# A decoder block in float32 pairs: right-hand SBUF pools moved from 96 to 64 bytes past multiples of 128, and the squares of the residual written two tiles back

## The chip, the cores and the metric

The kernel runs on one core of one Trainium2 chip. Its time is device microseconds from start to end of one execution; the number given for a kernel is the median of several executions. Engines are named as in the profile: PE multiplies matrices (PEld loads its stationary operand), DVE and ACT work element by element, POOL and SP mostly issue DMAs here.

## The reference

One layer of a decoder block, 512 tokens by 2048 features, all float32:

```python
h = rms_norm(x, g_mix)
x = x + concat(rms_norm(nsa(h)), gla(h)) @ w_out
x = x + cross_attention(rms_norm(x, g_cross), rms_norm(mem, g_mem)) @ w_co   # 4 heads, 256 memory tokens
hf = rms_norm(x, g_ffn)                                  # this x is "x2" below
gg, uu = split(hf @ w_gu)                                # 2048 -> 2 * 5632
return x + (silu(gg) * uu) @ w_down                      # 5632 -> 2048
```

## The kernel before

Every product that matters is a three-part product: each float32 operand is split into a high part (ACT, `S.copy` to fp32r) and a low part (DVE, source minus high part), in `split` (L186 and L187), and `mm3` issues three matmuls of 128x128 by 512 columns: high stationary with high moving, the same stationary with low moving, low stationary with high moving. This document calls these three a **triple**. All are recorded on L107. In a tile list such as `t<-qh,PB` the first name is the PSUM bank, the second the moving operand, the third the stationary one.

The stages, in order: projections of `mem` and `x` (`natural`, where the weights move and the tiles `X` are stationary; `project`, where the weights `wh`, `wl` are stationary and `X` moves), the attention groups, `w_out`, cross attention, then per 128-feature tile m the `w_co` product (`co_part`, both operands in right-hand pools), then the gate and up product in Strassen form (`phase`, `product`: split weights `qh`, `ql` move and the prepared activations `PA`, `PB` are stationary), and the down product (`down_product`, again `qh`, `ql` moving over `PB`).

SBUF is given out from both ends. Pools opened on the left (`const`, `sbb`, later `PA`, `PB`, `C`) start at multiples of 128 bytes in each partition, and so do nearly all their tiles; `X`, `PA`, `PB`, `C` all do. Pools opened with `side="right"` grow down from the top: first `sba` (`wh`, `wl`, `w`, `KS`, `KV`, `on`, `q1`, `rs`, `M`), later, in its place, the pool of `T2`, `qh`, `raw`, `ql`. By the sizes of the small tiles at the top, these tiles all start 96 bytes past a multiple of 128. So the two operands of a matmul start either 96 bytes (`qh` over `PB`) or 32 bytes (`X` over `wh`) apart, modulo 128, or at the same place (`M` over `wh`, both right; `P` over `Q` in cross attention, both left).

The stage around the second edit is the loop over the 16 tiles m of x2 (L1163 on). Tile m of the residual lies in `xs[m]`; which right-hand buffer that is, `X_AT` says. Per m: `co_part` on PE; DVE adds the residual into `xs[m]` (L1170); ACT's queue issues the store of `xs[m]` to DRAM (L1173); ACT scales it by the gain into half of a `PB` tile (`begin_combos`, L1111). Every second m, DVE and ACT build the sums and splits of that pair (`sums`, L1123 to L1126, then `split`), and PE does `unsummed`, 12 matmuls, for the pair before. `square(m - 2)` (L1157) squares `xs[m-2]` in place on ACT, which must wait until the store has read the tile, and POOL adds the square to one of two DRAM accumulators, `ssd`, by an accumulating DMA (L1159, L1161); each such DMA waits for the one before it on the same accumulator. Squares 14 and 15 come after the loop.

Then `first.close()` gives the right-hand buffers to `raw`, `qh` and `ql`, so that the first loads and splits of the FFN wait for what last used those bytes: the third `raw` tile lies over the buffers of x2's tiles 14 and 15. `phase` begins with a head: the weights of two slices, kp = 0 and 1, are loaded, and their products are written bank set by bank set, for each set first kp = 0 and then kp = 1. Instructions are ordered by a scheduler with priorities, so written order and engine order differ; the rows below are from the engine order.

Of the kernel before, what the change touches and what calls it, by code (L numbers as in the profile page):

```python
# [13 lines left out]
AF = mybir.ActivationFunctionType  # L14
OP = mybir.AluOpType
# [4 lines left out]
KT = D // 128  # L20
# [4 lines left out]
KP = KT // 2  # L25
NB = D_FF // 512
AHEAD = 150
# [16 lines left out]

FIRST_SUM, LAST_SUM = 70, 576

X_AT = ("KV", (3, 14, 12, 7, 13, 15, 2, 1, 0, 8)), ("KS", (11, 4, 5, 6)), ("q1", (9,)), ("on", (10,))
OC = "M", "M", "on", "KV"

SV = {}  # L50
# [10 lines left out]
def hybrid_block(ctx: ExitStack, tc: tile.TileContext, x_t, mem_t, sv, cmat, umask, w_a, w_r67, w_v, w_vg, w_v3,  # L61
                 w_vsw, w_gk2, w_c1, w_c2, w_out, w_cq, w_ck, w_cv, w_co, w_gu, w_down, y_t):
    nc = tc.nc
    V, S, G, PE = nc.vector, nc.scalar, nc.gpsimd, nc.tensor
# [11 lines left out]
    def sb(shape, tag, bufs, dt=F32):  # L76
        return (pool_b if tag in LATE else pool).tile(shape, dt, name=tag, tag=tag, bufs=bufs)
# [18 lines left out]
    def bank(tag):  # L96
        return psp.tile([128, 512], F32, name=tag, tag=tag, bufs={"mm": 3, "s": 2, "t": 2, "o": 1}[tag])
# [3 lines left out]
    def row(tag, dt=F32):  # L101
        return sb([128, 512], tag, BUFS[tag], dt)
# [125 lines left out]
    def mm3(ps, lhs, rhs, start, stop, again=False):  # L228
        mm(ps, lhs[0], rhs[0], start=start, stop=False, skip_group_check=again)
        mm(ps, lhs[0], rhs[1], start=False, stop=False, skip_group_check=again)  # L230
        mm(ps, lhs[1], rhs[0], start=False, stop=stop, skip_group_check=again)
# [255 lines left out]
    rs, rc = norm["row"], norm["col"]  # L487
# [480 lines left out]
    xs = [None] * KT  # L968
    for tag, ms in X_AT:
        for m in ms:  # L970
# [4 lines left out]
    for m in range(KT):  # L975
# [13 lines left out]
        else:  # L989
            sq = row("n")  # L990
# [73 lines left out]
    def co_part(ps, m, hs):  # L1064
        for h in hs:
            mm3(ps, co[m // 2](512 * (m % 2) + 128 * h, 128), oc[h], start=h == 0, stop=h == 3)

    co = [Weights(w_co[c], 1024, ahead=60) for c in range(2)]
    flows.until(lambda: len(oc) >= 3)
    ps4 = [bank(t) for t in ("mm", "mm", "mm", "s")]  # L1070
# [4 lines left out]
    flows.drain()  # L1075
    held.close()

    BUFS2 = {"T2": 8, "raw": 3, "qh": 5, "ql": 4, "PA": 16, "PB": 17, "C": 8}
    COLS2 = {"raw": 2048, "qh": 1024, "ql": 1024, "PB": 1280}
    pools2 = {}  # L1080

    def open_pool(names, **side):
        p = ctx.enter_context(tc.tile_pool(name="s" + names[0], bufs=1, reuse_waits="tile", **side))
        for n in names:
            pools2[n] = p
            sb2(n)

    def sb2(tag, dt=F32):
        return pools2[tag].tile([128, COLS2.get(tag, 512)], dt, name=tag, tag=tag, bufs=BUFS2[tag])

# [11 lines left out]
    ssd = [dram.tile([128, 512], F32, name="ss", tag="ss", bufs=2) for _ in range(2)]  # L1102
# [29 lines left out]
    def factor(kp, a, i):  # L1132

        return part(combos[kp][a > 1], 256 * (0, 1, 3, 4, 0, 1, 2)[a] + 128 * i, 128)

    def product(banks, kp, a, w, start, stop, again):
        for i in range(2):
            mm3(banks[i], factor(kp, a, i), w, start=start, stop=stop, again=again)
# [13 lines left out]
    def unsummed(kp):  # L1152
        for banks, a in ((b1, 0), (bp, 1)):
            product(banks, kp, a, wa[kp][a], kp == 0, kp == KP - 1, False)

    def square(m):
        S.activation(xs[m], xs[m], AF.Square)  # L1157
        if m < 2:
            G.dma_start(ssd[m], xs[m])  # L1159
        else:  # L1160
            G.dma_start(ssd[m % 2], xs[m], accum_op=OP.add)  # L1161

    for m in range(KT):  # L1163
        x = xs[m]
        if m < 4:
            ps = ps4[m]
        else:
            ps = bank("mm")
            co_part(ps, m, range(4))
        V.tensor_add(x, ps, x)  # L1170
        if m % 4 == 0:
            x2d.append(dram.tile([128, 2048], F32, name="x2", tag="x2", bufs=4))
        S.dma_start(x2d[-1][:, 512 * (m % 4):512 * (m % 4) + 512], x)  # L1173
        if m % 2 and m < 13:
            co.append(Weights(w_co[m // 2 + 2], 1024, ahead=60))
        begin_combos(m, x)
        if m % 2:
            wa[m // 2] = weights_a(m // 2)
            if m > 2:
                unsummed(m // 2 - 1)  # L1180
                sums(m // 2 - 1)()
        if m > 1:
            square(m - 2)
    for m in (KT - 2, KT - 1):
        square(m)
    unsummed(KP - 1)
    sums(KP - 1)()

    first.close()
    open_pool(("T2", "qh", "raw", "ql"), side="right")  # L1190
    open_pool(("C",))
    kept = [None] * KP

# [34 lines left out]
    PHASE_1 = (4, 0, 5, 3)  # L1228
    PHASE_2 = (1, 2, 6)

    def phase(load, banks, plan, middle, last, fresh, ahead, extra, fence=()):

        ws = {}

        def weights(kp):
            with tc.high_priority(offset=AHEAD if kp > 1 else ahead), ExitStack() as behind:
                if kp == 2:
                    for i in fence:
                        behind.enter_context(tc.issue_after(i.ins))
                ws[kp] = load(kp)  # L1240

        for kp in range(2):
            weights(kp)
        for p, a in enumerate(plan):
            for kp in range(2):
                product(banks[p], kp, a, ws[kp][p], fresh and kp == 0, False, not fresh)
        for kp in range(2, KP):
            weights(kp)
            for p in last if kp == KP - 1 else middle:
                product(banks[p], kp, plan[p], ws[kp][p], False, kp == KP - 1, not fresh)  # L1250
            for go in extra.get(kp, ()):
                go()
# [43 lines left out]
    fence = ()  # L1296
    for n in range(NB):
        if n == 0:
            u, c11 = [sb2("C") for _ in range(2)], [sb2("C") for _ in range(2)]
            with tc.high_priority(offset=2 * EVICT):  # L1300
                for i in range(2):
                    fa = S.copy(u[i], b1[i])
                for i in range(2):
                    fv = V.tensor_add(c11[i], u[i], bp[i])
            bu, b2, b3 = [bank("mm"), bank("mm")], [bank("mm"), bank("o")], [bank("t"), bank("t")]
            phase(weights_b, (bu, b2, b3), (4, 5, 3), (1, 2, 0), (0, 1, 2), True, AHEAD, {KP - 3: [norm_2]}, (fa, fv))
        else:
            b1 = c11 = [bank("mm"), bank("mm")]
            bu = [bank("s"), bank("s")]
            b2 = [bank("t"), bank("t")]  # L1310
            b3 = [bank("mm"), bank("o")]
            phase(lambda kp: weights_1(n, kp), (bu, b1, b2, b3), PHASE_1, (2, 3, 1, 0), (1, 0, 2, 3), True, AHEAD, {},
                  fence)
            u = [sb2("C") for _ in range(2)]
        c22 = [sb2("C") for _ in range(2)]
        with tc.high_priority(offset=EVICT):
            for i in range(2):
                if n:
                    fa = S.copy(u[i], b1[i])
                V.tensor_sub(u[i], u[i], bu[i])  # L1320
            for i in range(2):
                V.tensor_add(c22[i], u[i], b2[i])
            for i in range(2):
                fv = V.tensor_add(c22[i], c22[i], b3[i])
        extra = {}
        if hs:
            extra = {2: [turn(hs, n - 1, 0)], 4: [turn(hs, n - 1, 1)]}
        if n == 0:
            phase(weights_c, (b2, b3), (2, 6), (0, 1), (0, 1), False, AHEAD, {}, (fv,))
        else:  # L1330
            phase(lambda kp: weights_2(n, kp), (b1, b2, b3), PHASE_2, (1, 0, 2), (0, 1, 2), False, AHEAD, extra,
                  (fa, fv))
        g1, g2 = [sb2("C") for _ in range(2)], [sb2("C") for _ in range(2)]
        with tc.high_priority(offset=EVICT):
            for i in range(2):
                fa = S.activation(g1[i], c11[i], AF.Silu, scale=rc2[0][:, i:i + 1])
            for i in range(2):
                V.tensor_add(g2[i], u[i], b2[i])
            for i in range(2):
                fv = V.tensor_add(u[i], u[i], b3[i])  # L1340
        fence = fa, fv
        for i in range(2):
            S.activation(g2[i], g2[i], AF.Silu, scale=rc2[0][:, 2 + i:3 + i])
        for i in range(2):
            V.scalar_tensor_tensor(g1[i], u[i], rc2[1][:, i:i + 1], g1[i], op0=OP.mult, op1=OP.mult)
        for i in range(2):
            V.scalar_tensor_tensor(g2[i], c22[i], rc2[1][:, 2 + i:3 + i], g2[i], op0=OP.mult, op1=OP.mult)
        hs = g1 + g2
# [87 lines left out]
    banks = [None, [bank(t) for t in SETS[1]]]  # L1436
# [3 lines left out]
    for step, plan in enumerate(STEPS):  # L1440
# [3 lines left out]
        elif step == 1:  # L1444
            banks = [[bank(t) for t in SETS[r]] for r in rs_]
        elif step == 2:
            banks[1] = [bank(t) for t in SETS[1]]
        else:
            banks = [[bank(t) for t in SETS[r]] for r in rs_]
        for kp in range(NK):  # L1450
# [13 lines left out]
            if step == 0 and kp % 2 and 5 <= kp < 21:  # L1464
                for m in (kp - 5, kp - 4):
                    if m % 4 == 0:
                        raw = sb1("raw")
# [139 lines left out]
```

## Time and profile before

| what | us |
|---|---|
| median of 3 executions | 2365.82 (2364.24 to 2371.68) |
| the profiled execution | 2368.13 |
| its span, first to last instruction | 2366.3 |
| PE idle in front of matmuls, longest | 5.49, at 1057.9 |

The page of the profile gives busy time by engine, the chain of waits that ended last, and the costliest groups of instructions. A matmul's record lasts about 0.4 us, but the next one starts before it ends; the distance between the starts of neighbours, called **pitch** here, is what adds up to time. It is read from the timeline, whose first column is the start in us from the start of the span. The timeline merges equal neighbours into one row with a count.

### The profile page before, as it was taken

To read this page: it belongs to the slowest core of one execution; us is meant where nothing else is said; L and a number is where in the kernel's file an instruction comes from. 1 tells how busy PE (TensorE), PEld (TensorE's weight loads), DVE (VectorE), ACT (ScalarE), POOL (GpSimd) and SP (SyncE) were. 2 spreads that over 40 slices of the span, in tenths; PEclk is the share of its full clock that TensorE was granted. 3 is DMA by queue.
4 is the path that set the end of the run, shared out by engine and by line. 5 is a ranking of instruction groups with operands and counts; after the bars stand their busy time and mean duration, and the time that the engine had idled before them with its cause. 6 is when DMAs were issued, how large, how long until landed. Compare 5 with 4: busy or idle time off the path is not lost.

```text
span 2366.3 us, 29749 instructions
## 1 busy us (share of the span) xinstructions
PE 2345.7 (99%) x10962; PEld 1913.9 (81%) x10962; DVE 1663.5 (70%) x2523; ACT 1179.9 (50%) x1793; POOL 149.9 (6%) x200
## 2 busy tenths in 40 slices
PE   8999999999999999989999999999999999999999
PEld 7898887888887888778888888888888888878787
DVE  6637885666778335586788778878877876775685
ACT  6533454556667224474455444544554555444442
POOL 0011111111112110020000000000000000000000
PEclk9999999999999999999999999999999999999999
DMA  7487568865558773296345435544554397776773
GB/s 272 151 209 177 139 160 223 211 171 136 163 143 253 213 180 114 84 228 206 129 159 182 153 122 170 169 148 136 166 168 144 134 317 281 237 236 228 241 248 143
DMA packets 140995, 434.72 MB, mean 184 GB/s; under 512 B 14416, under 2 KB 34896, under 8 KB 137392
## 3 DMA queue, kind: packets, MB, share of 16 engines
q1 hardware_dynamic: 88528, 329.25, 41.9%
q0 software_dynamic: 28896, 79.18, 15.6%
q10 hardware_dynamic: 23424, 24.39, 3.0%
q8 instruction: 86, 1.41, 0.3%
q14 instruction: 61, 0.50, 0.1%
HBM read 394.22 MB, written 101.45 MB: 209 GB/s over the span
## 4 chain that ended last, share of the span: by engine, by line
PE 97%; DVE 1%; DMA 1%; ACT 1%; issue 0%; SPq 0%; DVEq 0%; ACTq 0%
PE mm L107 51%; PE t L107 18%; PE s L107 15%; PE o L107 10%; PE t L894 1%; PE s L1265 1%; DMA PH<-w_ck 0%; PE t L1415 0%; DMA st<-x_t 0%; DVE ql L187 0%; DMA st<-w_gk 0%; DMA ss<-KV 0%; PE t L882 0%; ACT PB L186 0%; DVE ss L467 0%
## 5 line engine op out<-in xcount | busy, mean ns | idle before, releaser
L186 ACT CAST qh<-raw 128x1024 fp32r<-128x1024 f32 x498 | 481.4, 976 | 545.8 <-PE o L107 177.6
L187 DVE TENSOR_TENSOR ql<-raw,qh 128x1024 fp32r<-128x1024 f32 x498 | 558.2, 1127 | 194.5 <-PE mm L107 46.9
L107 PE MATMUL mm<-X,wh 128*128 128x512 f32 x1664 | 533.8, 401 | 0.0
L107 PEld LDWEIGHTS mm<-X,wh 128*128 128x128 f32 x1664 | 305.8, 189 | 66.0 <-issue 1.7
L107 PE MATMUL t<-qh,PB 128*128 128x512 f32 x968 | 339.1, 395 | 0.0
L107 PE MATMUL mm<-X,wl 128*128 128x512 f32 x832 | 330.3, 397 | 0.0
L187 DVE TENSOR_TENSOR wl<-w,wh 128x1024 fp32r<-128x1024 f32 (+2 forms) x172 | 205.9, 1202 | 158.9 <-ACT wh L186 157.0
L107 PE MATMUL mm<-qh,PB 128*128 128x512 f32 x868 | 314.9, 395 | 0.0
L186 ACT CAST wh<-w 128x1024 fp32r<-128x1024 f32 (+2 forms) x172 | 176.3, 1030 | 265.4 <-PE mm L107 170.1
L107 PE MATMUL s<-qh,PB 128*128 128x512 f32 x672 | 235.7, 395 | 0.0
L107 PE MATMUL mm<-qh,PA 128*128 128x512 f32 x640 | 224.3, 394 | 0.0
L107 PEld LDWEIGHTS t<-qh,PB 128*128 128x128 f32 x968 | 181.8, 188 | 44.5
L107 PEld LDWEIGHTS mm<-qh,PB 128*128 128x128 f32 x868 | 163.7, 189 | 40.7 <-ACT qh L186 0.4
L107 PE MATMUL o<-qh,PB 128*128 128x512 f32 x484 | 190.1, 394 | 5.5 <-ACT qh L186 5.5
L107 PE MATMUL t<-ql,PB 128*128 128x512 f32 x484 | 192.8, 398 | 0.0
L107 PEld LDWEIGHTS mm<-X,wl 128*128 128x128 f32 x832 | 156.6, 188 | 37.7 <-DVE wl L187 1.2
L107 PE MATMUL mm<-ql,PB 128*128 128x512 f32 x434 | 173.1, 399 | 1.0 <-DVE ql L187 1.0
L107 PEld LDWEIGHTS s<-qh,PB 128*128 128x128 f32 x672 | 126.2, 188 | 30.7
L107 PEld LDWEIGHTS mm<-qh,PA 128*128 128x128 f32 x640 | 120.2, 188 | 29.9
L107 PE MATMUL s<-ql,PB 128*128 128x512 f32 x336 | 133.9, 398 | 0.2 <-DVE ql L187 0.2
L107 PE MATMUL mm<-ql,PA 128*128 128x512 f32 x320 | 127.5, 399 | 0.0
L107 PEld LDWEIGHTS o<-qh,PB 128*128 128x128 f32 x484 | 91.0, 188 | 28.5 <-ACT qh L186 5.9
(456 smaller groups left out, 3431.6 us busy)
## 6 DMA issues: line engine op xcount, KB each, us to landing
raw<-w_gu SPq DMA_DIRECT2D x80, 768.0 KB, 4.2
raw<-w_down SPq DMA_DIRECT2D x88, 512.0 KB, 4.6
raw<-w_gu SPq DMA_DIRECT2D x80, 512.0 KB, 3.6
td<-w_down POOLq DMA_DIRECT2D x66, 512.0 KB, 7.1
w<-w_a SPq DMA_DIRECT2D x60, 512.0 KB, 5.4
raw<-td SPq DMA_DIRECT2D x22, 1024.0 KB, 4.8
PB<-h SPq DMA_DIRECT2D x35, 512.0 KB, 4.3
h<-T ACTq DMA_DIRECT2D x66, 256.0 KB, 3.6
```

The lines of the kernel that those rows point to most:

```text
L107: last_mm[0] = PE.matmul(*args, **kw)
L186: S.copy(hi, src)
L187: V.tensor_sub(lo, src, hi)
L894: PE.transpose(tp[:, 128 * (i - j):128 * (i - j) + 128], ps_[b][:, POFF[i] + 128 * j:POFF[i] + 128 * j + 128], ident)
L1265: PE.transpose(ps[f][:, 128 * i:128 * i + 128], hs[i][:, c:c + 128], ident)
```

## The change

Four edits. `pad` is a tile of 32 bytes in each of the two right-hand pools; it is never written or read, and lets everything below it start 64 bytes past a multiple of 128 instead of 96. `square(m)` runs in iteration m itself and writes into the buffer of tile m-2 (for m = 0 and 1 into a free row). `X_AT` exchanges the buffers of tiles 12 to 15, so that the third `raw` tile now lies over tiles 12 and 13, into which squares 14 and 15 go. In the first FFN phase alone, the head goes through all three bank sets for kp = 0 and then for kp = 1 (`by_pair`).

```diff
-X_AT = ("KV", (3, 14, 12, 7, 13, 15, 2, 1, 0, 8)), ("KS", (11, 4, 5, 6)), ("q1", (9,)), ("on", (10,))
+X_AT = ("KV", (3, 12, 14, 7, 15, 13, 2, 1, 0, 8)), ("KS", (11, 4, 5, 6)), ("q1", (9,)), ("on", (10,))
...
+    sb([128, 8], "pad", 1)
     co = [Weights(w_co[c], 1024, ahead=60) for c in range(2)]
...
-    BUFS2 = {"T2": 8, "raw": 3, "qh": 5, "ql": 4, "PA": 16, "PB": 17, "C": 8}
-    COLS2 = {"raw": 2048, "qh": 1024, "ql": 1024, "PB": 1280}
+    BUFS2 = {"T2": 8, "raw": 3, "qh": 5, "ql": 4, "PA": 16, "PB": 17, "C": 8, "pad": 1}
+    COLS2 = {"raw": 2048, "qh": 1024, "ql": 1024, "PB": 1280, "pad": 8}
...
     def square(m):
-        S.activation(xs[m], xs[m], AF.Square)
+        sq = xs[m - 2] if m > 1 else row(("rs", "q1")[m])
+        S.activation(sq, xs[m], AF.Square)
         if m < 2:
-            G.dma_start(ssd[m], xs[m])
+            G.dma_start(ssd[m], sq)
         else:
-            G.dma_start(ssd[m % 2], xs[m], accum_op=OP.add)
+            G.dma_start(ssd[m % 2], sq, accum_op=OP.add)
...
-        if m > 1:
-            square(m - 2)
-    for m in (KT - 2, KT - 1):
         square(m)
...
-    open_pool(("T2", "qh", "raw", "ql"), side="right")
+    open_pool(("T2", "qh", "raw", "ql", "pad"), side="right")
...
-        for p, a in enumerate(plan):
-            for kp in range(2):
-                product(banks[p], kp, a, ws[kp][p], fresh and kp == 0, False, not fresh)
+        head = [(p, kp) for p in range(len(plan)) for kp in range(2)]
+        for p, kp in sorted(head, key=lambda h: h[1]) if by_pair else head:
+            product(banks[p], kp, plan[p], ws[kp][p], fresh and kp == 0, False, not fresh)
```

ACT at the end of the loop over m, before; `KV_7114` and `KV_7122` hold tiles 14 and 15, `PB_9303` and `PB_9371` are the last two pairs, `C` the first evictions of the FFN:

```order
L1111 ACTIVATE PB_9371<-KV_7114,vecs_113 128x512
L1157 ACTIVATE KV_7116<-KV_7116 128x512
L1173 DMA x2_9301<-KV_7122 128x512
L1111 ACTIVATE PB_9371<-KV_7122,vecs_113 128x512
L1157 ACTIVATE KV_7120<-KV_7120 128x512
L186 CAST PA_9391<-PB_9371 128x512
L186 CAST PB_9418<-PB_9303 128x1280
L1157 ACTIVATE KV_7114<-KV_7114 128x512
L1157 ACTIVATE KV_7122<-KV_7122 128x512
L186 CAST PB_9444<-PB_9371 128x1280
L1302 COPY C_9466<-t_8912 128x512
L1302 COPY C_9467<-t_8913 128x512
```

The same place now; `KV_7116` and `KV_7120` hold tiles 14 and 15, `PB_9310` and `PB_9378` are the last two pairs:

```order
L1159 ACTIVATE KS_7132<-KV_7122 128x512
L1175 DMA x2_9308<-KV_7116 128x512
L1112 ACTIVATE PB_9378<-KV_7116,vecs_113 128x512
L1159 ACTIVATE KV_7114<-KV_7116 128x512
L1175 DMA x2_9308<-KV_7120 128x512
L1112 ACTIVATE PB_9378<-KV_7120,vecs_113 128x512
L186 CAST PB_9425<-PB_9310 128x1280
L186 CAST PA_9398<-PB_9378 128x512
L1159 ACTIVATE KV_7122<-KV_7120 128x512
L186 CAST PB_9447<-PB_9378 128x1280
L1301 COPY C_9470<-t_8913 128x512
L1301 COPY C_9471<-t_8914 128x512
```

Two squares fewer stand between the last scaled tile and the last cast, the last square no longer overwrites the tile that was just sent to DRAM, and the wide cast of pair 6 now stands ahead of the cast of pair 7.

PE in the head of the first FFN phase, before; `qh_9486`, `ql_9487`, `qh_9482`, `ql_9483` are weights of kp = 0, `qh_9496` and `ql_9497` of kp = 1:

```order
L107 MATMUL mm_9474<-ql_9487,PB_8983 128x512
L107 MATMUL mm_9474<-qh_9486,PB_8984 128x512
L107 MATMUL mm_9475<-ql_9487,PB_8983 128x512
L107 MATMUL mm_9475<-qh_9486,PB_8984 128x512
L107 MATMUL mm_9474<-qh_9496,PB_9058 128x512
L107 MATMUL mm_9475<-qh_9496,PB_9058 128x512
L107 MATMUL mm_9476<-ql_9483,PB_8983 128x512
L107 MATMUL mm_9474<-ql_9497,PB_9058 128x512
```

The same place now; `qh_9490`, `ql_9491`, `qh_9486`, `ql_9487` are weights of kp = 0, `qh_9500` of kp = 1:

```order
L107 MATMUL mm_9480<-qh_9486,PB_8991 128x512
L107 MATMUL o_9481<-ql_9487,PB_8990 128x512
L107 MATMUL o_9481<-qh_9486,PB_8991 128x512
L107 MATMUL t_9482<-qh_9486,PB_8990 128x512
L107 MATMUL t_9482<-ql_9487,PB_8990 128x512
L107 MATMUL t_9482<-qh_9486,PB_8991 128x512
L107 MATMUL t_9483<-qh_9486,PB_8990 128x512
L107 MATMUL t_9483<-ql_9487,PB_8990 128x512
L107 MATMUL t_9483<-qh_9486,PB_8991 128x512
L107 MATMUL mm_9478<-qh_9500,PB_9065 128x512
```

The first matmul that needs kp = 1 has moved from the ninth place of the head to the nineteenth.

More of the change, by code (lines that the diff above doesn't have):

```diff
@@ L1229, in hybrid_block, with phase @@
     PHASE_2 = (1, 2, 6)
-    def phase(load, banks, plan, middle, last, fresh, ahead, extra, fence=()):
+    def phase(load, banks, plan, middle, last, fresh, ahead, extra, fence=(), by_pair=False):
         ws = {}
@@ L1305, in hybrid_block @@
             bu, b2, b3 = [bank("mm"), bank("mm")], [bank("mm"), bank("o")], [bank("t"), bank("t")]
-            phase(weights_b, (bu, b2, b3), (4, 5, 3), (1, 2, 0), (0, 1, 2), True, AHEAD, {KP - 3: [norm_2]}, (fa, fv))
+            phase(weights_b, (bu, b2, b3), (4, 5, 3), (1, 2, 0), (0, 1, 2), True, AHEAD, {KP - 3: [norm_2]}, (fa, fv),
+                  True)
         else:
```

## The prediction

> **What bounds the kernel now.** The page first: the span, the busy time of PE, and the chain that ended last.
>
> ```profile
> span 2366.3 us, 29749 instructions
> PE 2345.7 (99%) x10962; PEld 1913.9 (81%) x10962; DVE 1663.5 (70%) x2523; ACT 1179.9 (50%) x1793; POOL 149.9 (6%) x200
> PE 97%; DVE 1%; DMA 1%; ACT 1%; issue 0%; SPq 0%; DVEq 0%; ACTq 0%
> ```
>
> PE is busy from end to end and carries 97% of the chain, so waits can give back about 20 us at most. More can come only from the pitch of the matmuls. The timeline gives it; in each pair of rows below I count the matmuls from the first start to the second.
>
> ```profile
> 1232.52 0.39 PE L107 MATMUL t<-qh,PB 128*128 128x512 f32 x1
> 1239.52 0.39 PE L107 MATMUL s<-qh,PB 128*128 128x512 f32 x1
> ...
> 849.77 0.63 PE L107 MATMUL mm<-X,wh 128*128 128x512 f32 x2
> 857.51 0.63 PE L107 MATMUL mm<-X,wh 128*128 128x512 f32 x2
> ...
> 1034.53 0.61 PE L107 MATMUL mm<-KV,wh 128*128 128x512 f32 x2
> 1037.25 0.61 PE L107 MATMUL mm<-KV,wh 128*128 128x512 f32 x2
> ```
>
> In the FFN (right-hand moving operand, left-hand stationary one, 96 bytes apart modulo 128), 30 matmuls take 7.00 us: 0.700 us for a triple. In the projections (left moving, right stationary, 32 apart), 33 take 7.74: 0.7036 for a triple. In the `w_co` stage (both right-hand, 0 apart), 12 take 2.72: 0.680 for a triple. All have 512 columns. So where the two operands start at the same place modulo 128, a triple is 20 to 24 ns shorter. Is that something else, such as other engines or DMAs at work beside it? Two stretches of the FFN, by windows (columns: stretch, length, busy time and count of PE, PEld, DVE, ACT, POOL, clock, DMA share, GB/s):
>
> ```profile
> 1225.00:1250.00 25.00, 25.00 (x108) 20.10 (x108) 16.44 (x21) 9.58 (x13) 0.00 (x0) 1.00 0.28 95
> 2050.00:2075.00 25.00, 25.00 (x108) 20.10 (x108) 17.71 (x15) 11.50 (x11) 0.00 (x0) 1.00 0.74 248
> ```
>
> DMA share 0.28 or 0.74, the same 108 matmuls: the pitch does not follow the traffic. It belongs to the operands' placement, and the first edit alters exactly that.
>
> **The pad.** It adds no instruction. Everything right-hand moves from 96 to 64 bytes past a multiple of 128; left-hand tiles stay. Pairs that lay 96 or 32 apart now lie 64 apart; pairs within one side stay 0 apart. How many triples that touches is read from the groups, where a triple has two matmuls with the high moving or stationary part (`qh`, `wh`):
>
> ```profile
> L107 PE MATMUL t<-qh,PB 128*128 128x512 f32 x968 | 339.1, 395 | 0.0
> L107 PE MATMUL mm<-qh,PB 128*128 128x512 f32 x868 | 314.9, 395 | 0.0
> L107 PE MATMUL s<-qh,PB 128*128 128x512 f32 x672 | 235.7, 395 | 0.0
> L107 PE MATMUL mm<-qh,PA 128*128 128x512 f32 x640 | 224.3, 394 | 0.0
> L107 PE MATMUL o<-qh,PB 128*128 128x512 f32 x484 | 190.1, 394 | 5.5 <-ACT qh L186 5.5
> L107 PE MATMUL mm<-X,wh 128*128 128x512 f32 x1664 | 533.8, 401 | 0.0
> L107 PE MATMUL mm<-wh,X 128*128 128x512 f32 x224 | 80.8, 403 | 6.2 <-ACT wh L186 6.0
> L107 PE MATMUL o<-wh,X 128*128 128x512 f32 x96 | 39.1, 407 | 0.0
> ```
>
> FFN and down product: (968 + 868 + 672 + 640 + 484) / 2 = 1816 triples. `X` over `wh`: 832. `wh` over `X`: (224 + 96) / 2 = 160, taken like the FFN.
>
> No row shows two operands 64 apart, so the new pitch has to be bounded. The nearest rows are 0 apart (0.680) and 32 or 96 apart (0.700, 0.7036). Downwards, a triple could come to 0.680: 1976 x 0.020 + 832 x 0.0236 = 39.5 + 19.6 = **59 us** gained. In the middle, 64 apart could cost what 32 and 96 cost: nothing gained. Upwards, the cost could grow with the distance, 64 being as far as two places modulo 128 can be: twice the excess, 59 us lost. I take the lower bound, 59 us gained. The reason is what the excess does at 0, 32 and 96: none, 24 ns and 20 ns. If operands are read in pieces of 64 bytes, both neighbours of 0 are half a piece out of step, and 64 is in step again, like 0. The size fits: 20 ns a triple is 6.7 ns a matmul, and from the next rows 256 more columns take 226.7 - 118.3 = 108.4 ns, so that 16 columns, which are 64 bytes, take 6.8. Against it stand the same rows, with 256 columns, where placement hardly matters:
>
> ```profile
> 983.64 1.59 PE L107 MATMUL s<-P,Q 128*128 128x256 f32 x12
> 985.06 0.40 PE L107 MATMUL mm<-M,wh 128*128 128x512 f32 x1
> ...
> 112.11 0.40 PE L107 MATMUL t<-wh,X 128*128 128x256 f32 x2
> 113.91 0.28 PE L107 MATMUL t<-wh,X 128*128 128x256 f32 x1
> ```
>
> Both left-hand: 12 in 1.42 us, 118 ns each; 96 apart: 15 in 1.80, 120 ns each. So I count nothing for narrower matmuls, and the middle bound keeps a real chance.
>
> DVE and ACT have 30% and 50% of the span free; a PE that is 2.5% faster raises DVE from 70% to 72%. In the FFN window above DVE has 16.44 of 25 us, so the splits keep ahead. I count no new waits.
>
> The Trainium skill's page "SBUF — State Buffer", section "Who interferes with whom", gives PE two independent read ports, one for the moving operand and one for the weights, and says that PE never waits on anyone. By that, placement could not matter and this edit would give nothing, which is the first rival below. The rows of this trace, 0.680 beside 0.700 for equal shapes, speak against it.
>
> **The squares, `X_AT` and the head.** They act at one place, the handover to the FFN, where PE has its longest idle time. The timeline there:
>
> ```profile
> 1047.54 0.72 ACT L1111 ACTIVATE PB<-KV,vecs 128x512 f32<-128x512 f32 x1 [1.48 <-DVE PB L1123]
> 1048.69 0.60 ACT L186 CAST PA<-PB 128x512 fp32r<-128x512 f32 x1
> 1049.19 1.26 ACT L186 CAST PB<-PB 128x1280 fp32r<-128x1280 f32 x1
> 1052.04 0.40 PE L107 MATMUL s<-wh,PA 128*128 128x512 f32 x1
> 1050.73 0.42 DVE L1126 TENSOR_TENSOR PB<-PB 128x256 f32<-128x256 f32 x1
> 1054.17 0.63 ACT L1157 ACTIVATE KV<-KV 128x512 f32<-128x512 f32 x1 [3.19 <-DMA x<-KV]
> 1054.71 1.24 ACT L186 CAST PB<-PB 128x1280 fp32r<-128x1280 f32 x1
> 1055.86 1.06 ACT L1302 COPY C<-t 128x512 f32<-128x512 f32 x2
> 1055.98 1.49 DVE L187 TENSOR_TENSOR PB<-PB 128x1280 fp32r<-128x1280 f32 x1 [3.42 <-ACT PB L186]
> 1056.81 3.04 ACT L186 CAST qh<-raw 128x1024 fp32r<-128x1024 f32 x4
> 1057.39 1.28 DVE L1304 TENSOR_TENSOR C<-C,s 128x512 f32<-128x512 f32 x2
> 1057.92 0.80 PE L107 MATMUL o<-qh,PB 128*128 128x512 f32 x1 [5.49 <-ACT qh L186]
> 1058.59 3.56 DVE L187 TENSOR_TENSOR ql<-raw,qh 128x1024 fp32r<-128x1024 f32 x4
> 1060.46 0.79 PE L107 MATMUL mm<-ql,PB 128*128 128x512 f32 x1 [0.38 <-DVE ql L187]
> 1061.29 7.78 SPq L1216 DMA_DIRECT2D raw<-gu  x4
> ```
>
> ACT stands 3.19 us before square 15, which may not overwrite tile 15 until its store has read it. Behind it in ACT's queue wait the last cast of `PB`, the two copies and the first `qh`, and PE waits for `qh`. Now square 15 goes over tile 13, whose store was issued two tiles earlier, and this wait goes. What is late next? By the order rows, the cast of pair 6 (1.26 us) stands ahead of pair 7's. From the end of the last scaled tile at 1048.3: cast of pair 6 to 1049.5, cast of `PA` (0.60) to 1050.1. DVE: low part of pair 6 (1.49 as the row of pair 7) from 1049.5 to 1051.0, low part of `PA` (512 of 1280 columns of such a step, about 0.7) to 1051.7, the two sums that are left (0.42 each) to 1052.5. ACT: cast of pair 7 (1.24) to 1053.8, copies (1.06) to 1054.9, first `qh` (3.04 / 4) to 1055.6. PE then starts the FFN at 1055.7 instead of 1057.92. Its next condition, `ql`, follows DVE: low part of pair 7 from 1053.8 to 1055.3, the two additions (1.28) to 1056.6, two `ql` (half of the 3.56 of four) to 1058.4, against 1060.46. So 2.0 to 2.2 us: I take **2 us**. Bounds: 0, if another wait takes the place; and 8 us, if all goes:
>
> ```profile
> 1052.00:1058.00 6.00, 0.51 (x3) 0.08 (x1) 2.58 (x4) 3.83 (x6) 1.70 (x2) 0.80 0.81 141
> 1058.00:1062.40 4.40, 4.03 (x9) 2.59 (x10) 4.14 (x6) 1.85 (x3) 1.13 (x2) 0.50 0.78 135
> ```
>
> After the idle time the clock stands at 0.50 for 4.40 us, and 9 matmuls run where 19 would at 0.233 (a third of 0.700): some 2.2 us lost on top of the 5.49 and 0.38. Whether an idle time of 2.6 us (1053.1 to 1055.7) brings the half clock too, the trace doesn't say; I assume it does.
>
> The Trainium skill's page "TensorE: Matmul & The Clock Gate", section "HAM oscillation — how this bites in real kernels", names an idle gap above about 3.4 us as what halves the clock. The 5.49 us and the 0.50 above agree. By that rule a gap of 2.6 us would keep the full clock, and the sum would be 2 us better.
>
> The squares themselves cost what they did: 16 on ACT, 16 DMAs on POOL. A square into the buffer of tile m-2 waits for the store of tile m-2, the same condition as before, two tiles after the store; only the last pair is spared. The third `raw` (SP row, 1061.29) waits for the last accumulating DMA; with squares 14 and 15 some 3 us earlier it comes earlier too. It costs nothing in either kernel: the head's 36 matmuls, 8.4 us, hide it, since PE shows no idle time after 1060.46. The head by kp only moves the need for kp = 1 back, worth at most the 0.38 already counted: nothing.
>
> **The sum.** 59 + 2 = 61 us. Against the profiled execution, 2368.13 with its span of 2366.3, that is 2307; the median of the runs shown is 2365.82, 0.1% lower, and I apply the sum to it: **2305 us**.
>
> **Rivals.** *Placement does not matter at 64, or not as I think* (the 0.680 belongs to both operands being right-hand, or 64 costs what 32 costs): only the handover stays, 2364. For it: the 256-column rows. Against: nothing else differs between the 0.680 and the 0.700. *Only one direction gains*, since the moving operand may count otherwise than the stationary one: FFN alone 2365.8 - 39.5 - 2 = 2324, projections alone 2344; between them 2334. *64 is the worst place* (slower): if the pieces are of 128 bytes, half a piece out of step is 64, the excess doubles to 40 and 47 ns a triple, and the time is 2365.8 + 59 - 2 = 2423. It decides as soon as an FFN triple takes more than 0.700. For it: the excess rises from 0 to 32, and nothing in the trace shows it fall again before 96. Against: the same excess at 32 and 96, and its size of 16 columns.
>
> **How the numbers follow.** Forecast 0.62, no effect of placement 0.16, one direction 0.10, worst place 0.12. The range takes the forecast with its bounds (2305 - 6 for a handover that vanishes, 3 more for rounding of the pitches: 2296), one direction, and no effect with its noise, to 2368: 0.88 of the chance; without the no-effect case 0.72 would be left. A measurement of this kernel can tell about 0.3%, 7 us, from no change. Faster by more: 0.62 + 0.10 = 0.72. Within: 0.16. Slower: 0.12.
>
> **What would show it.** In the FFN, windows of 25 us with 111 or 112 matmuls instead of 108 and a triple of 0.680 in the timeline; the same in the projections; `w_co` unchanged. At the handover no wait of ACT for the store before the last square, and an idle time of PE of about 2.6 us. The prediction is wrong if the FFN triple stays at 0.700 or grows, or if DVE or ACT turn up as what PE waits for in the FFN.

## The result: 23 us gained instead of 61

| kernel | median, us | lowest to highest | ratio to the kernel before, 95% |
|---|---|---|---|
| before, beside it on the same chip | 2366.23 (4 runs) | 2364.24 to 2371.68 | 1 |
| changed kernel | 2343.17 (4 runs) | 2338.98 to 2344.93 | 0.9896 (0.9875 to 0.9918) |

The change gains 1.0%, 23 us. The direction was forecast and the time lies in the range, but the forecast 2305 is 38 us off. The page of the changed kernel's profile, its three lines that answer to those of before:

```profile
span 2342.4 us, 29747 instructions
PE 2318.8 (99%) x10962; PEld 1910.7 (82%) x10962; DVE 1660.5 (71%) x2523; ACT 1178.7 (50%) x1793; POOL 149.9 (6%) x200
PE 94%; DMA 2%; DVE 2%; ACT 1%; issue 1%; SPq 0%; DVEq 0%; ACTq 0%
```

PE still bounds the kernel, with the same 10962 matmuls. Its busy time fell by 26.9 us, and its share of the chain fell from 97% to 94%: some waits have appeared. The pitch is read from the timeline as before, two rows for each stage, from one start to another (FFN, projections, `w_co`):

```profile
1226.32 0.39 PE L107 MATMUL t<-qh,PB 128*128 128x512 f32 x1
1233.19 0.39 PE L107 MATMUL s<-qh,PB 128*128 128x512 f32 x1
...
845.65 0.63 PE L107 MATMUL mm<-X,wh 128*128 128x512 f32 x2
852.65 0.63 PE L107 MATMUL mm<-X,wh 128*128 128x512 f32 x2
...
1031.09 0.62 PE L107 MATMUL mm<-M,wh 128*128 128x512 f32 x2
1033.81 0.39 PE L107 MATMUL mm<-M,wh 128*128 128x512 f32 x1
```

In the FFN 30 matmuls take 6.87 us: a triple of 0.687, where 0.700 stood before and 0.680 was forecast. In the projections 30 take 7.00: 0.700, where 0.7036 stood and 0.680 was forecast. In `w_co` 12 still take 2.72: 0.680, as forecast. So 64 bytes apart is cheaper than 96 in one stage and hardly cheaper in the other, and in neither is it in step.

Where time came back is in the groups of instructions (busy us, mean ns, then idle us before them and its releaser):

```profile
L107 PE MATMUL o<-qh,PB 128*128 128x512 f32 x484 | 189.2, 393 | 2.7 <-ACT qh L186 2.7
L107 PE MATMUL mm<-ql,PB 128*128 128x512 f32 x434 | 171.0, 394 | 2.3 <-DVE ql L187 2.3
L107 PE MATMUL s<-ql,PB 128*128 128x512 f32 x336 | 132.2, 393 | 0.9 <-DVE ql L187 0.9
L107 PE MATMUL t<-wh,PA 128*128 128x512 f32 x32 | 11.5, 401 | 1.7 <-ACT PA L186 1.7
```

The two groups with `ql`, before:

```profile
L107 PE MATMUL mm<-ql,PB 128*128 128x512 f32 x434 | 173.1, 399 | 1.0 <-DVE ql L187 1.0
L107 PE MATMUL s<-ql,PB 128*128 128x512 f32 x336 | 133.9, 398 | 0.2 <-DVE ql L187 0.2
```

The wait for the first `qh` fell from 5.5 to 2.7 us. In exchange PE now waits 1.7 for a cast of `PA`, and the waits for `ql` grew from 1.0 to 2.3 and from 0.2 to 0.9.

### The profile page after: what moved, and what is told of

Read it like the earlier page. It is cut to its first block, busy times and chain, and to the rows that moved or that the text cites. A ratio compares the mean times of both kernels' runs of the same rounds, so it can differ in the third digit from the quotient of the medians.

```text
span 2342.4 us, 29747 instructions
## 1 busy us (share of the span) xinstructions
PE 2318.8 (99%) x10962; PEld 1910.7 (82%) x10962; DVE 1660.5 (71%) x2523; ACT 1178.7 (50%) x1793; POOL 149.9 (6%) x200
## 4 chain that ended last, share of the span: by engine, by line
PE 94%; DMA 2%; DVE 2%; ACT 1%; issue 1%; SPq 0%; DVEq 0%; ACTq 0%
PE mm L107 50%; PE t L107 17%; PE s L107 15%; PE o L107 10%; PE t L894 1%; PE s L1264 1%; DMA PB<-h 1%; DVE ql L187 1%; DMA raw<-w_gu 0%; DMA h<-T 0%; DMA st<-x_t 0%; PE t L1415 0%; DMA PH<-w_ck 0%; ACT wh L186 0%; DMA st<-w_gk 0%
## 5 line engine op out<-in xcount | busy, mean ns | idle before, releaser
L187 DVE TENSOR_TENSOR ql<-raw,qh 128x1024 fp32r<-128x1024 f32 x498 | 558.2, 1127 | 180.6 <-PE mm L107 45.7
L107 PE MATMUL mm<-X,wh 128*128 128x512 f32 x1664 | 532.5, 400 | 0.0
L107 PEld LDWEIGHTS mm<-X,wh 128*128 128x128 f32 x1664 | 304.9, 188 | 65.6 <-issue 1.7
L107 PE MATMUL t<-qh,PB 128*128 128x512 f32 x968 | 338.0, 394 | 0.0
L107 PE MATMUL mm<-X,wl 128*128 128x512 f32 x832 | 329.6, 396 | 0.1
L187 DVE TENSOR_TENSOR wl<-w,wh 128x1024 fp32r<-128x1024 f32 (+2 forms) x172 | 205.9, 1202 | 157.7 <-ACT wh L186 157.2
L107 PE MATMUL mm<-qh,PB 128*128 128x512 f32 x868 | 312.6, 393 | 0.1
L107 PE MATMUL s<-qh,PB 128*128 128x512 f32 x672 | 234.0, 393 | 0.0
L107 PE MATMUL mm<-qh,PA 128*128 128x512 f32 x640 | 223.2, 392 | 0.0
L107 PEld LDWEIGHTS t<-qh,PB 128*128 128x128 f32 x968 | 182.4, 188 | 39.3
L107 PEld LDWEIGHTS mm<-qh,PB 128*128 128x128 f32 x868 | 163.4, 188 | 36.6 <-ACT qh L186 0.5
L107 PE MATMUL o<-qh,PB 128*128 128x512 f32 x484 | 189.2, 393 | 2.7 <-ACT qh L186 2.7
L107 PE MATMUL t<-ql,PB 128*128 128x512 f32 x484 | 189.6, 392 | 0.0
L107 PEld LDWEIGHTS mm<-X,wl 128*128 128x128 f32 x832 | 156.3, 188 | 37.6 <-DVE wl L187 1.3
L107 PE MATMUL mm<-ql,PB 128*128 128x512 f32 x434 | 171.0, 394 | 2.3 <-DVE ql L187 2.3
L107 PEld LDWEIGHTS s<-qh,PB 128*128 128x128 f32 x672 | 126.2, 188 | 27.0
L107 PEld LDWEIGHTS mm<-qh,PA 128*128 128x128 f32 x640 | 120.2, 188 | 26.1
L107 PE MATMUL s<-ql,PB 128*128 128x512 f32 x336 | 132.2, 393 | 0.9 <-DVE ql L187 0.9
L107 PE MATMUL mm<-ql,PA 128*128 128x512 f32 x320 | 124.7, 390 | 0.0
L107 PEld LDWEIGHTS o<-qh,PB 128*128 128x128 f32 x484 | 91.1, 188 | 22.9 <-ACT qh L186 3.1
```

Of the source, the lines that this page charges most:

```text
L107: last_mm[0] = PE.matmul(*args, **kw)
L187: V.tensor_sub(lo, src, hi)
```

## The experiments

Where a tile starts follows from the order of the allocations: left-hand tiles start 128 past a multiple of 256, right-hand ones 224 less the pad. So before, the moving operand started 96 after the stationary one in the FFN, and 160 after it modulo 256 (32 modulo 128) in the projections. The times beside which each ran are 2368.06 (first four, 19 runs of the kernel before), 2367.70 (next four, 13) and 2367.87 (last three, 13).

### Which part of the change carries it

The kernel before with the pads alone (e1), and the changed kernel without them (e2):

```diff
 # e1, against the kernel before
+    sb([128, 8], "pad", 1)
...
-    open_pool(("T2", "qh", "raw", "ql"), side="right")
+    open_pool(("T2", "qh", "raw", "ql", "pad"), side="right")
 # e2, against the changed kernel: the same lines taken out
```

> The kernel before with the 32-byte pads alone; squares, X_AT and head as before. If the placement carries the whole change (the FFN triple at 0.687 us instead of 0.700, 1816 triples, so about 23 us, and about 4 us ahead of the FFN), the time is 2341 to 2345 us, the same as the whole change. If the handover edits carry a share as well (2 to 6 us), it is 2345 to 2350 us.

> The whole change without the pads: right-hand tiles stay 96 bytes past multiples of 128. If the handover is worth the 2 us of the forecast, the time is about 2 us under the kernel before (2364); if the new wait ahead of the last unsummed products takes it back, it is within 1 us of the kernel before. If the pads' gain hung on these edits, it would be 2 us or more above it.

Measured: e1 2344.51 (0.9902, 0.9887 to 0.9917), e2 2367.10 (0.9998, 0.9989 to 1.0008). The placement carries the whole gain, and the squares, `X_AT` and the head by kp carry nothing that these times can tell (e2's interval reaches from 2.6 us gained to 1.9 lost). The handover in e2, where the placement is that of before, by timeline. The first row is the last `w_co` matmul, the last row the 37th matmul of the FFN, the first behind the head:

```profile
1044.26 0.40 PE L107 MATMUL mm<-KV,wl 128*128 128x512 f32 x1
1044.90 0.68 DVE L187 TENSOR_TENSOR PA<-PB,PA 128x512 fp32r<-128x512 f32 x1
1045.50 0.68 DVE L1171 TENSOR_TENSOR KV<-mm,KV 128x512 f32<-128x512 f32 x1
1046.59 0.73 ACT L1111 ACTIVATE PB<-KV,vecs 128x512 f32<-128x512 f32 x1 [1.69 <-DVE PB L1125]
1047.22 1.24 ACT L186 CAST PB<-PB 128x1280 fp32r<-128x1280 f32 x1
1048.37 0.61 ACT L186 CAST PA<-PB 128x512 fp32r<-128x512 f32 x1
1048.89 0.63 ACT L1158 ACTIVATE KV<-KV 128x512 f32<-128x512 f32 x1
1049.04 0.50 PE L107 MATMUL t<-wh,PA 128*128 128x512 f32 x1 [1.58 <-ACT PA L186]
1051.54 1.26 ACT L186 CAST PB<-PB 128x1280 fp32r<-128x1280 f32 x1 [2.03 <-DVE PB L1126]
1054.77 0.79 PE L107 MATMUL o<-qh,PB 128*128 128x512 f32 x1 [2.67 <-ACT qh L186]
1057.31 0.80 PE L107 MATMUL mm<-ql,PB 128*128 128x512 f32 x1 [0.38 <-DVE ql L187]
1066.70 0.40 PE L107 MATMUL mm<-qh,PB 128*128 128x512 f32 x1
```

Of before, the rows that answer to its first, third and last:

```profile
1046.01 0.40 PE L107 MATMUL mm<-KV,wl 128*128 128x512 f32 x1
1046.44 0.69 DVE L1170 TENSOR_TENSOR KV<-mm,KV 128x512 f32<-128x512 f32 x1
1068.91 0.39 PE L107 MATMUL mm<-qh,PB 128*128 128x512 f32 x1
```

The windows of the half clock, before and in e2 (columns as in the prediction):

```profile
1055.61:1062.43 6.82, 4.13 (x9) 2.70 (x10) 6.16 (x7) 4.24 (x7) 2.10 (x4) 0.50 0.78 123
1054.48:1061.30 6.82, 6.15 (x13) 4.29 (x14) 4.51 (x6) 2.71 (x5) 0.56 (x1) 0.50 0.92 291
```

The last square starts without a wait, where ACT stood 3.19 us before. From the start of the last `w_co` matmul to the first of the FFN PE takes 11.91 us before and 10.51 here: 1.4 saved. To the 37th matmul of the FFN it takes 22.90 and 22.44: only 0.5 is left.

The clock takes the rest. It stands at 0.50 for 6.8 us in both kernels. Before, the first 2.3 of them fell into PE's idle time ahead of 1057.92; in e2 only 0.3 did, so that more of the head runs at half clock. The other kernels below show the same. With the squares, `X_AT` and the head of the change, whatever the pads, the first FFN matmul comes 10.5 to 10.6 us after the last of `w_co`; without them 11.9 to 12.2 (in e6, where PE's idle time is 3.57 us, 9.95). The 37th comes after 22.4 to 23.3 with them, and after 22.8 to 23.2 without. It is clearly earlier, at 22.0, only in e7, e8 and e9, where the half clock lasted 3.4 us instead of 6.8.

### How the time goes with the distance

In e3, e4 and e7 to e11 only the number of bytes in the two pads changes (the width in `sb([128, 8], "pad", 1)` and in `"pad": 8`, in elements of 4 bytes): 96 puts right-hand tiles on multiples of 128 like the left-hand ones, and 64 puts them 32 past.

> The change with pads of 96 bytes: right-hand tiles on multiples of 128, so that all operands lie 0 apart modulo 128. If distance modulo 128 sets the pitch, the FFN triple and the projections' triple come to 0.680 us as in the w_co stage, and the time to about 2316 us (1976 x 7 ns and 832 x 20 ns under the change's 2343). If the 0.680 belongs to operands of the same side and not to the distance, the FFN triple stays between 0.687 and 0.700, time 2340 to 2366 us.

> The change with pads of 64 bytes: right-hand tiles 32 past multiples of 128, so the FFN's operands lie 32 apart and the projections' 96, the mirror image of the kernel before. If the excess depends on the distance alone and not on which operand is ahead, the FFN triple is 0.7036 us as the projections' was, time about 2370 us; if it depends on whether right-hand tiles start on a multiple of 64 bytes, it is 0.700 us; if direction matters otherwise, some third value.

Measured: e3 2324.57 (0.9818, 0.9802 to 0.9835), e4 2364.07 (0.9983, 0.9974 to 0.9992). The timelines, 30 matmuls in each pair of rows, FFN and projections of e3:

```profile
1225.88 0.39 PE L107 MATMUL o<-qh,PB 128*128 128x512 f32 x1
1232.68 0.39 PE L107 MATMUL o<-qh,PB 128*128 128x512 f32 x1
...
840.06 0.62 PE L107 MATMUL mm<-X,wh 128*128 128x512 f32 x2
846.86 0.62 PE L107 MATMUL mm<-X,wh 128*128 128x512 f32 x2
```

6.80 us in both: 0.680 a triple. What `w_co` shows in every kernel is had everywhere once all operands start at the same place, and the kernel is faster than both others, though 8.6 us above the 2316 that was expected. e4 has 7.00 in both, like the FFN before. So the step of the prediction that made the pitch a matter of placement stands. The 43.5 us are still less than the 59 worked out for all triples at 0.680; the section on the prediction says where the rest is, as far as the rows show it.

### Is it the distance, or each operand's own start?

In e3 everything also lies on multiples of 128. In e6 everything lies 96 past them: the kernel before, with a tile of 96 bytes put in front of the left-hand pools. e5 is the kernel before with pads of 96 alone, without the other edits.

```diff
 # e6, against the kernel before
     const = ctx.enter_context(tc.tile_pool(name="const", bufs=1))
+    const.tile([128, 24], F32, name="pad")
```

> The kernel before with 96 bytes in front of the left-hand pools and no pad on the right: now left-hand and right-hand tiles all start 96 past a multiple of 128, 0 apart but aligned to nothing above 32. Theory (only the distance modulo 128 counts): an FFN triple of 0.680 us, 2324.6 as with everything on multiples of 128. Rival (an operand that does not start on a multiple of 64 or 128 costs by itself): triples of 0.700 in the FFN and in the projections, 2350 to 2370.

> The kernel before with the right-hand pools on multiples of 128 (pads of 96 bytes) and nothing else of the change: squares, X_AT and head as before. If placement is all that counts, the time is that of the pad of 96 with the handover edits, 2324.6, within 3 us, and PE has its single wait of more than 5 us at the start of the FFN again. If the handover edits are worth the 2 us of the prediction once PE is faster, 2326.6 or more.

Measured: e6 2324.76 (0.9819, 0.9805 to 0.9834), e5 2323.51 (0.9814, 0.9799 to 0.9828). The FFN of e6 (the added line moves L107 to L108):

```profile
1226.03 0.39 PE L108 MATMUL s<-ql,PB 128*128 128x512 f32 x1
1232.83 0.39 PE L108 MATMUL t<-ql,PB 128*128 128x512 f32 x1
```

6.80 us again, with no operand on a multiple of 64. At the starts tried here only the distance counts, not what the starts are multiples of. This also answers e4, whose 0.700 its expectation would have put down to a rule of multiples of 64. And e5, which leaves the handover as it was, with PE's idle time of 5.64 us at the start of the FFN, is as fast as e3 within the noise of some 3 us: no gain of the other edits shows with the faster PE either.

### After how many bytes does it repeat?

e7 has pads of 224 bytes: 0 apart modulo 128, but 128 apart modulo 256. e9 has pads of 352: 0 apart modulo 512, where e3 and e6 are 256 apart.

> The changed kernel with pads of 224 bytes: right-hand tiles on multiples of 256, left-hand ones 128 past them, so 0 apart modulo 128 and 128 apart modulo 256. Theory (the pattern repeats every 128 bytes): FFN triple 0.680, 2324.6. Rival (it repeats every 256 bytes or later): 128 apart is as far as two places can be, FFN triple 0.687 to 0.700 or more, 2344 to 2368.

> The changed kernel with pads of 352 bytes: left-hand and right-hand tiles now 0 apart modulo 512; with pads of 96, and with 96 in front of the left-hand pools, they were 0 apart modulo 256 but 256 apart modulo 512. Theory (the pattern repeats every 256 bytes): FFN triple 0.680 and 2324.6 again. Rival (it repeats every 512 bytes): another triple than 0.680, below it (0.660, under 2300) or above (0.687 to 0.700, 2340 to 2368).

Measured: e7 2358.39 (0.9960, 0.9946 to 0.9975), e9 2325.42 (0.9815, 0.9800 to 0.9830). FFN and projections of e7:

```profile
1225.84 0.39 PE L107 MATMUL t<-qh,PB 128*128 128x512 f32 x1
1232.81 0.39 PE L107 MATMUL s<-qh,PB 128*128 128x512 f32 x1
...
840.20 0.62 PE L107 MATMUL mm<-X,wh 128*128 128x512 f32 x2
847.17 0.62 PE L107 MATMUL mm<-X,wh 128*128 128x512 f32 x2
```

6.97 us in both stages: at 128 apart nearly the whole excess is there, so 128 is not the period. The theory that I took into the experiments, distance modulo 128, falls here. e9's FFN:

```profile
1225.85 0.39 PE L107 MATMUL mm<-ql,PA 128*128 128x512 f32 x1
1232.65 0.39 PE L107 MATMUL t<-ql,PB 128*128 128x512 f32 x1
```

6.80 us, as at 256 apart: 0 and 256 are alike, and the distances are counted modulo 256 from here on.

### Which of the two operands is ahead

In the changed kernel 64 apart gave 0.687 in the FFN and 0.700 in the projections. Modulo 256 these aren't the same distance: the moving operand starts 64 after the stationary one in the FFN and 192 after it in the projections. e10, with pads of 160, exchanges the two; e11, with 192, gives 160 and 96; e8, with 112, gives 240 and 16.

> The changed kernel with pads of 160 bytes. In the FFN the moving operand now starts 192 bytes after the stationary one modulo 256 (64 in the changed kernel), in the projections 64 (192 in the changed kernel): the two distances are exchanged. Theory A (what counts is how far the moving operand starts after the stationary one): the triples are exchanged too, FFN 0.700, projections 0.687, some 2358. Theory B (what counts is only how far apart they are, or the FFN and the projections differ for another reason): FFN 0.687, projections 0.700, 2343.

> The changed kernel with pads of 192 bytes: in the FFN the moving operand starts 160 bytes after the stationary one modulo 256, in the projections 96. From the projections of the kernel before (160 after: 0.702) and its FFN (96 after: 0.700), Theory A expects FFN 0.702, projections 0.700, 2362 to 2368; a theory by which 160 is nearer than 192 to something good would show below 0.695 and under 2355.

> The changed kernel with pads of 112 bytes: right-hand tiles 112 past multiples of 128, 16 bytes apart from the left-hand ones. Theory A (any start that is not the same modulo 128 costs the step of 20 ns a triple, 64 excepted): FFN triple 0.700, about 2364. Theory B (the cost grows with the distance up to 32): about 0.690 and 2345. Theory C (reads go in pieces of 32 bytes, and within one piece a distance costs nothing): 0.680 and 2325.

Measured: e10 2358.33 (0.9957, 0.9941 to 0.9974), e11 2369.70 (1.0008, 0.9999 to 1.0018), e8 2365.47 (0.9989, 0.9980 to 0.9999). FFN and projections of e10:

```profile
1226.02 0.63 PE L107 MATMUL mm<-qh,PA 128*128 128x512 f32 x2
1233.02 0.39 PE L107 MATMUL mm<-qh,PB 128*128 128x512 f32 x1
...
840.76 0.62 PE L107 MATMUL mm<-X,wh 128*128 128x512 f32 x2
847.63 0.62 PE L107 MATMUL mm<-X,wh 128*128 128x512 f32 x2
```

7.00 and 6.87: the two stages have exchanged their pitches along with their distances. So how far the moving operand starts after the stationary one, modulo 256, sets the pitch, and not the stage. In e8 both stages show 7.00, so 16 bytes already cost as much as 32 (Theory A of its expectation). e11 has 7.03 and 7.00, as Theory A has it, and its time is 1.7 us above the 2368 expected. All eleven experiments and the two kernels together, us for 30 matmuls of 512 columns, read in each timeline as above:

| moving after stationary, bytes modulo 256 | FFN | projections |
|---|---|---|
| 0 (e3, e5, e6, e9) | 6.80 | 6.80 |
| 16 | | 7.00 (e8) |
| 32 | 7.00 (e4) | |
| 64 | 6.87 (changed, e1) | 6.87 (e10) |
| 96 | 7.00 (before, e2) | 7.00 (e11) |
| 128 | 6.97 (e7) | 6.97 (e7) |
| 160 | 7.03 (e11) | 7.03 (before, e2) |
| 192 | 7.00 (e10) | 7.00 (changed, e1) |
| 224 | | 7.00 (e4) |
| 240 | 7.00 (e8) | |

Wherever both stages were tried at one distance, they agree to 0.01 us. The projections in which `wh` moves over `X` lie as far apart as the FFN and agree with it too, but for e7: there 30 of their matmuls take 7.00 us (75.42 to 82.42) against 6.97. Why is open.

## Why the prediction was wrong, and where it was right

**The pad, direction and cause: right.** The pitch goes by how the two operands lie to each other, the traffic beside it does not matter, and `w_co` does not change. e1 and e2 show that nothing else in the change counts by more than their noise. The first rival, no effect of placement, is refuted by e3 and e5. The Trainium skill's page "SBUF — State Buffer", section "Who interferes with whom", gives PE two independent read ports. e5 has the instructions of the kernel before and takes 0.9814 of its time, so those reads are not independent of each other's addresses here.

**The pad, size: wrong.** The step that failed is "If operands are read in pieces of 64 bytes, both neighbours of 0 are half a piece out of step, and 64 is in step again, like 0". I had reduced all addresses modulo 128 without a row that shows such a period, and thrown the sign of the distance away. Both were wrong: the period is 256, the projections stood at 160 rather than 32, and their new 192 is no mirror image of the FFN's 64. At 64 the excess over 0.680 is 0.007 of 0.020 and not nothing. The terms with what they measured:

- FFN and `wh` over `X`: 1976 triples at 0.013 are 25.7 us instead of 39.5.
- Projections: 832 triples at 0.703 - 0.700 are 2.5 us instead of 19.6. That term all but vanished. (The 0.7036 came from rows that are rounded to 0.01 us; the table's 7.03 is 0.703.)
- Handover: 0.3 us lost in the changed kernel (23.22 us from the last `w_co` matmul to the 37th of the FFN, against 22.90), where 2 gained were forecast; 0.5 gained in e2 (below).
- New waits, which I had counted at nothing. Behind the 37th matmul of the FFN, the waits of 0.1 us and more in front of matmuls add up to 0.8 us before and 3.3 in the changed kernel, the largest at the row below: 2.5 us lost. They are 3.6 in e1 and 1.3 in e2, so most of them come with the faster PE.

```profile
1912.01 0.77 PE L1264 MATMUL t<-ident,C 128*128 128x128 f32 x5 [1.23 <-DVE C L1347]
```

Together 25.7 + 2.5 - 0.3 - 2.5 = 25.4 us, against 23.9 by the two spans and 23 by the medians. The 1.5 us between are less than what separates executions of one kernel (2338.98 to 2344.93) and are not assigned.

**The bounds were sound.** "In the middle" (64 costs what 32 costs) and "downwards" (0.680) enclosed what came, 0.687 and 0.700. The fault was to take one end because one explanation fitted four rows. The rival that the pitch depends on direction was there with 0.10, as a matter of the stage, and its time for the projections alone, 2344, is the measured one by accident: in fact the FFN gained and the projections did not. A time that matches a rival does not confirm it; the rows do.

**At 0 apart, 59 us were still too many.** e3 gains 43.5. In dense stretches of the projections a triple falls by 0.023, about as worked out. But 59 also supposes that every triple stands among its like; the projections between the attention groups fall less (medians by stretches of 50 us from 500 to 750 us: 702 to 703 ns before, 690 to 691 in e3). Up to the start of the FFN e3 has gained 1057.92 - 1043.55 = 14.4 us, where 22.8 were worked out, and behind it 28.6, where 1816 x 0.020 are 36.3. Of these last 7.7, 2.2 are waits (3.0 us behind the head against 0.8 before); the rest is not assigned.

**The handover: the chain was right, its start and the clock were not.** ACT's wait for the store went, and the idle time before the first `qh` was forecast as 2.6 and is 2.67 in e2, 2.69 in the changed kernel. From the end of the last scaled tile to the first FFN matmul the prediction counted 7.4 us (1048.3 to 1055.7); e2 takes 7.45 (1046.59 + 0.73 to 1054.77). What I had missed lies ahead of that chain and behind it. Ahead: DVE's residual add for tile 15 (L1171) stands behind the low parts of a pair (L187). In the new order these end later, at 1045.58 in e2, and the add starts 1.24 us after the last `w_co` matmul began instead of 0.43. So of the 2.2 us at the first FFN matmul 1.4 are left. Behind: I set the half clock's loss equal in both kernels, taking its length to be the 4.40 us that PE worked in it. It stood for 6.8 us in both, and what the shorter wait saves, more matmuls at half clock take back. The new wait of 1.58 to 1.70 us for the cast of `PA` is not lost on top: it comes out of the idle time ahead of the FFN, whose first matmul waits for ACT's `qh` and not for PE. The changed kernel's own rows:

```profile
1044.80 1.24 ACT L186 CAST PB<-PB 128x1280 fp32r<-128x1280 f32 x1
1045.95 0.61 ACT L186 CAST PA<-PB 128x512 fp32r<-128x512 f32 x1
1046.62 0.50 PE L107 MATMUL t<-wh,PA 128*128 128x512 f32 x1 [1.70 <-ACT PA L186]
1052.35 0.51 PE L107 MATMUL o<-qh,PB 128*128 128x512 f32 x1 [2.69 <-ACT qh L186]
1054.89 0.79 PE L107 MATMUL mm<-ql,PB 128*128 128x512 f32 x1 [1.05 <-DVE ql L187]
```

The wait for `ql` is 1.05 here and 0.38 before, but the matmul behind it starts 2.54 us after the first of the FFN in both: here PE was at full clock until 1053.88 and only reached it sooner.

That the half clock would come after 2.6 us was assumed, and it came. The Trainium skill's page "TensorE: Matmul & The Clock Gate", section "HAM oscillation — how this bites in real kernels", names gaps above about 3.4 us; in e2 the longest was 2.67 and the granted clock 0.50, so by this run shorter gaps can bring it too. The gap of 1.58 ends 3.1 us before that one begins (1049.04 and 1054.77 - 2.67); whether the two add up was not tried.

**Left open.** Why 64 is better than 96 or 128, and 160 the worst, no run settles. The runs show which distances cost how much, and not what in the chip makes them cost.

## What to carry to other kernels

Where a kernel is bound by matmuls, let the moving and the stationary operand start at the same address modulo 256: here a pad of 96 bytes alone gave 1.9%, and the three pairs of starts tried at 0 apart (e3 and e5, e6, e9) gave the same 6.80 us. Measure the pitch over some 30 matmuls in a steady stretch of each stage, and list it against the signed distance of the two operands; take no period for granted that the rows do not show. And when a wait goes, count what it saves from an instruction ahead of it that stands at the same place in both orders, follow what was let ahead in the queues of all engines that feed the chain, and look at the granted clock behind it.

## What the runs showed that was not expected

- 512-column fp32r matmuls take 226.7 ns each at 0 apart, 229 at 64 after, 232 at 128 (233.3 there for `wh` over `X`), 233.3 at 16, 32, 96, 192, 224 and 240, and 234.3 at 160: five values over ten distances.
- The half clock came at the handover in every kernel, with idle times of 2.67 to 5.77 us in front of the first `qh`. It stood for 6.8 us in ten of the thirteen and for 3.4 in e7, e8 and e9, whose idle time of 2.7 is that of kernels with 6.8.
- A pad 32 bytes narrower or 16 wider than the best one costs nearly all of the gain: from 2324.57 at 96 to 2364.07 at 64 and 2365.47 at 112.
